# Two-layer hybrid encoder trunk on one core: group C's score products cut into two column parts, opening transfers and one table step put in another order

## The chip, the cores and the metric

The kernel runs on one core of a Trainium2 chip. The metric is device time in microseconds (us) of one execution; lower is better. TensorE (PE) multiplies, VectorE (DVE), ScalarE (ACT) and GpSimd (POOL) work elementwise, SyncE (SP) issues most of the transfers.

## The reference, cut to what matters

Two layers over 256 tokens of width 2048, all in float32. Each layer makes one projection, three groups of attention heads, a gate, an output projection and a normalised residual:

```
h = rms_norm(x, g_pre)
proj = h @ w_in                  # columns: group A, group B (low rank), group C, gates
o_a = dense attention, 8 query heads, 2 key heads, rotary, q and k normalised
o_b = low-rank attention, 4 heads, shared rotary key
o_c = neighbourhood attention, 4 heads: token t is row t // 64, column t % 64 of a grid;
      a query sees 4 rows and 16 columns around its own, plus a learned bias
y = concat(o_a, o_b, o_c) * silu(gates) @ w_out
x = x + rms_norm(y, g_post)
```

The kernel computes group C densely: all 256 keys for each query, with a bias table that holds -1e30 where the neighbourhood doesn't reach.

## The kernel before, in words

Every float32 operand is split into a high part (rounded to the reduced float32 that TensorE takes in one pass; "fp32r" in the rows) and a low part, the rest. A product of two such operands is three products on TensorE: high by high, high by low, low by high (`mm3`). Each product loads its own 128x128 stationary operand (a weight load, PEld in the rows) and streams the other one through, 512, 320 or 256 columns wide; transposes stream 128.

Weights come in tiles of 128x1024 in the order of a fixed list (`CHUNKS`), through four raw buffers (`RAW_BUFS`), issued on SP. `conv` splits a tile: ACT casts it to the high part (`whi`, line 206), DVE subtracts for the low part (`wlo`, line 207). `feed` keeps casts a few tiles ahead of the products. A chunk opens with PSUM tiles named `mm` (four buffers, two for most chunks), its products are issued, and a task (`post_...`) reads the PSUM out later; tasks advance by steps, between the products of later chunks. The order of the first chunks of layer 0 is bcq (96 products, 8 weight tiles), bckv (96 products of 320 columns), gB.0, gB.1, and so on. gB.0 takes the two PSUM tiles that bcq leaves, gB.1 those of bckv.

The opening (`start`): the input comes transposed in four pieces `xT[0]` to `xT[3]` (512 KB each); each piece is scaled by `g_pre` and split into `hT` (ACT line 209 high, DVE line 210 low, four blocks a piece). `token_factors(0)` squares the four pieces (ACT), sums them, and gets the per-token factor r with a power on POOL (line 218); r stands in every `post_` task that reads the first chunks (`while (l, "r") not in self.done`). `rstd` uses the same power on POOL.

`layer_consts(l)` loads small constants and makes four rotary tables on POOL (`c_aqn`, `s_aqn`, `c_akn`, `s_akn`, lines 327 and 329) from a rotary table (`pr`) and two gains (`g_aqn`, `g_akn`), all of them brought in on SP's queue. The tables are first used by group A (akv, aq0), long after gB. In layer 0 it is called after the sixth weight tile (`i == 5`).

A head (`head`) makes its scores into one PSUM tile `sc`, two query halves of 128 by 256 keys; in groups A and C that is 2 x 3 = 6 products of 256 columns. Group C has 4 heads a layer, 8 in all.

The order of instructions on each engine is set by a scheduler from the order and priority in the program; each engine then runs its own list in order and waits on semaphores.

Of the kernel before, what the change touches and what calls it, by code (L numbers as in the profile page):

```python
# [8 lines left out]
AF = mybir.ActivationFunctionType  # L9
# [3 lines left out]
P = 128  # L13
# [5 lines left out]
GRID_W = 64  # L19
# [143 lines left out]
class Build:  # L163
# [147 lines left out]
    def layer_consts(self, l):  # L311
        nc, d = self.nc, self.d
        g = self.tmp("gq", [P, 512], bufs=1)
        nc.sync.dma_start(g, d["bqn"][l].partition_broadcast(P))
        self.g_bq = g
        g = self.tmp("gkv", [P, 256], bufs=1)
        nc.sync.dma_start(g, d["bkvn"][l].partition_broadcast(P))
        self.g_bkv = g
        self.tab = {}
        ra = self.tmp("pr", [P, 2, 256], bufs=2)  # L320
        nc.sync.dma_start(ra, self.rope_in[:, :, :256])
        for nme in ("aqn", "akn"):
            g = self.tmp("g_" + nme, [P, 128], bufs=1)
            nc.sync.dma_start(g, d[nme][l].partition_broadcast(P))
            c = self.tmp("c_" + nme, [P, 2, 128])
            s = self.tmp("s_" + nme, [P, 2, 128])
            nc.gpsimd.tensor_tensor(c, ra[:, :, :128], g.unsqueeze(1).to_broadcast([P, 2, 128]), ALU.mult)
            for h in range(2):
                nc.gpsimd.tensor_tensor(s[:, :, 64 * h:64 * h + 64], ra[:, :, 128 + 64 * h:192 + 64 * h],
                                        g[:, 64 - 64 * h:128 - 64 * h].unsqueeze(1).to_broadcast([P, 2, 64]), ALU.mult)  # L330
            self.tab[nme] = (c, s)
# [321 lines left out]
    def head(self, l, grp, h):  # L653
        nc = self.nc
        sp = self.psum("sc", 1)
        s3 = sp.rearrange("p (q k) -> p q k", q=2)
        for qt in range(2):
            q = slice(qt * P, (qt + 1) * P)
            st = qt == 0
            if grp == "A":  # L660
                qq, kk, kv = self.qA[h // 4], self.kA, h // 4
                self.mm3(s3[:, qt], qq[0][:, h % 4, q], qq[1][:, h % 4, q], kk[0][:, kv], kk[1][:, kv], st, True)
            elif grp == "C":
                qq, kk = self.qC, self.kC
                self.mm3(s3[:, qt], qq[0][:, h, q], qq[1][:, h, q], kk[0][:, h], kk[1][:, h], st, True)
            else:
                qq, kk = self.qn, self.kn
                self.mm3(s3[:, qt], qq[0][:, h, q], qq[1][:, h, q], kk[0][:, h], kk[1][:, h], st, False)
                self.mm(s3[:, qt], self.qpe[:, h, q], self.kpe, False, False)
                self.mm(s3[:, qt], self.qpe[:, h, q], self.kpl[:, h % 2], False, True)  # L670
        yield 1
        pr = self.tmp("pr", [P, 2, 256], bufs=2)
        mx = self.tmp("mx", [P, 2], bufs=2)
        nb = self.tmp("nb", [P, 2], bufs=2)
        sm = self.tmp("sm", [P, 2], bufs=2)
        rc = self.tmp("rc", [P, 2], bufs=2)
        if grp == "C":
            for qt in range(2):
                nc.vector.scalar_tensor_tensor(pr[:, qt], s3[:, qt], self.r[:, 2 + qt:3 + qt], self.biasC[h // 2][:, h % 2, qt], ALU.mult, ALU.add)
            nc.vector.reduce_max(mx, pr, AX.X)  # L680
            nc.vector.tensor_scalar(nb, mx, -1.0, None, ALU.mult)
            for qt in range(2):
                nc.scalar.activation(pr[:, qt], pr[:, qt], AF.Exp, bias=nb[:, qt:qt + 1], scale=1.0, accum_out=sm[:, qt:qt + 1])
        else:
            nc.vector.reduce_max(mx, s3, AX.X)
            if grp == "A":
                sc = self.scA[h // 4]
                nc.vector.scalar_tensor_tensor(nb, mx, -1.0, sc[:, :, h % 4], ALU.mult, ALU.mult)  # L688
            else:
                nc.vector.tensor_scalar(nb, mx, -(192 ** -0.5), None, ALU.mult)  # L690
            for qt in range(2):
                scale = sc[:, qt, h % 4:h % 4 + 1] if grp == "A" else 192 ** -0.5
                nc.scalar.activation(pr[:, qt], s3[:, qt], AF.Exp, bias=nb[:, qt:qt + 1], scale=scale, accum_out=sm[:, qt:qt + 1])  # L693
        yield 1
        nc.vector.reciprocal(rc, sm)
        for qt in range(2):
            nc.vector.tensor_scalar(pr[:, qt], pr[:, qt], rc[:, qt:qt + 1], None, ALU.mult)
        yield 2
        pt = self.psum("tr", 2)
        for qt in range(2):  # L700
            for kt in range(2):
                self.transpose(pt[:, kt * 256 + qt * P:kt * 256 + (qt + 1) * P], pr[:, qt, kt * P:(kt + 1) * P])
        yield 1
        pT = self.tmp("pT", [P, 2, 2, 256], bufs=1)
        self.split(pt.rearrange("p (k q) -> p k q", k=2), pT[:, 0], pT[:, 1])
        yield 2
        while grp == "C" and (l, "cv") not in self.done:
            yield 1
        po = self.psum("pv", 1)
        for kt in range(2):  # L710
            if grp == "A":
                c = slice((h // 4) * P, (h // 4 + 1) * P)
                v = self.vA
            else:
                c = slice(h * P, (h + 1) * P)
                v = self.vB if grp == "B" else self.vC
            self.mm3(po[:, :256], v[0][:, kt, c], v[1][:, kt, c], pT[:, 0, kt], pT[:, 1, kt], kt == 0, kt == 1)
        yield 1
        if grp == "C":
            nc.scalar.copy(self.oC[:, h], po[:, :256])  # L720
            return
        g = {"A": lambda: self.gA[h // 4][:, h % 4], "B": lambda: self.gB[:, h]}[grp]()
        og = self.tmp("og", [P, 256], bufs=1)
        nc.vector.scalar_tensor_tensor(og, po[:, :256], 0.5, g, ALU.mult, ALU.mult)
        e = {"A": h, "B": 8 + h}[grp]
        nc.scalar.copy(self.oT[0][:, e].bitcast(F32R), og)
        nc.vector.tensor_tensor(self.oT[1][:, e].bitcast(F32R), og, self.oT[0][:, e], ALU.subtract)
# [191 lines left out]
    def start(self):  # L919
# [10 lines left out]
        self.g_pre = self.pc.tile([P, KT], F32, name="g_pre")  # L930
        xT = self.xT0 = self.unit(3) + self.unit(4)
        with self.tc.high_priority(offset=1000):
            nc.sync.dma_start(self.g_pre, self.d["gpre0"])
            x0 = lambda a, b: nc.sync.dma_start(xT[0][:, a:b], self.xT[0][:, a:b])
            x0(0, 256)
            self.load(0, self.items[0]["ncols"], lambda: x0(256, 512))
            self.load(1)
            x0(512, 1024)
            nc.sync.dma_start(xT[1], self.xT[1])
            self.load(2)  # L940
            self.load(3)
            nc.sync.dma_start(xT[2], self.xT[2])
        self.nload = 4
        self.ident = self.pc.tile([P, P], F32, name="ident")
        self.rope = self.pc.tile([P, 2, 128], F32, name="rope")
        self.mhalf = self.pc.tile([P, 8], F32, name="mhalf")
        nc.vector.memset(self.mhalf, -0.5)
        one = self.tmp("rs_a", [P, 8], bufs=2)
        nc.vector.memset(one, 1.0)
        two = self.tmp("rs_r", [P, 8], bufs=4)  # L950
        nc.gpsimd.tensor_tensor(two, one, self.mhalf, ALU.pow)
        nc.scalar.activation(two, one, AF.Exp)
        self.new_layer()
        for c in range(4):
            v = xT[c].rearrange("p (k t) -> p k t", k=4)
            for j in range(4):
                k = 4 * c + j
                self.split(v[:, j], self.hT[c][:, j, 0], self.hT[c][:, j, 1], self.g_pre[:, k:k + 1])
                if j % 2:
                    self.feed(2 * c + j // 2, 0, 0)  # L960
            if c == 1:
                nc.sync.dma_start(xT[3], self.xT[3])

    def last_chunk(self, i):

# [129 lines left out]
                nc.sync.dma_start(self.x1[m][:, h * 1024:(h + 1) * 1024], self.xt[m][h])  # L1095
        self.spawn(self.token_factors(l + 1), delay=0)
        self.layer_consts(l + 1)
        self.close_chunk(C[0])

    def run(self):  # L1100
        self.start()
        i, n = 0, len(self.items)
        while i < n:
            self.step += 1
            it = self.items[i]
            if it["name"] == "y3":
                self.last_chunk(i)
                i += 14
                continue

            self.feed(i, i, LC + min(HELD, it["ks"][0] // 2) if it["name"] == "y2" else LC)
            if it["first"]:
                self.open_chunk(it)
            self.products(it)
            if i == 5:
                self.layer_consts(0)
            if i == 2:
                self.spawn(self.token_factors(0), delay=2)
            if it["last"]:
                self.close_chunk(it)  # L1120
            self.run_tasks()
            i += 1
# [40 lines left out]
```

## Time and profile before

| what | us |
|---|---|
| median of 3 runs | 814.95 (813.52 to 815.0) |
| profiled execution | 815.99 |
| its span in the profile | 814.1 |
| PE busy in the span | 802.9 |
| DVE, ACT, POOL busy | 562.6, 436.4, 37.9 |

Busy time of PE counts an instruction until its modelled end; products overlap each other's ends, so the distance from one start to the next is what a product costs. In a timeline a row gives the start, the time from the first start to the last end, and the number of instructions merged into it.

### The profile page before, as it was taken

What the parts mean: (1) busy time and instruction counts of PE and PEld (TensorE: products, weight loads), DVE (VectorE), ACT (ScalarE), POOL (GpSimd) and SP (SyncE); (2) the same over time, 40 slices, a digit from 0 to 9 for tenths busy, and PEclk for the clock granted to TensorE, in tenths of its full rate; (3) what the DMA queues carried; (4) which work ended last, traced back from release to release, by engine and by line L of the source; (5) the groups of instructions that cost most, each with busy time, mean ns of one, the idle gap of its engine ahead of it and who ended that gap; (6) DMA issues with size and microseconds to landing.
All of it is one profiled execution on the core that took longest, in us unless ns stands there. A gap on an engine that the chain in (4) does not pass through costs nothing.

```text
span 814.1 us, 11731 instructions
## 1 busy us (share of the span) xinstructions
PE 802.9 (99%) x4345; PEld 693.1 (85%) x4345; DVE 562.6 (69%) x887; ACT 436.4 (54%) x755; POOL 37.9 (5%) x55
## 2 busy tenths in 40 slices
PE   8999999999999999999999999999999999999996
PEld 5889888888898888888898898888889988888885
DVE  6767877576777687566595776866758866874643
ACT  7455555464665555456284554645456555554531
POOL 1110000000000000200010000001000000000000
PEclk9999999999999999999999999999999999999999
DMA  8775544554445455777367455446554455566632
GB/s 290 244 253 174 200 170 161 212 203 161 170 165 181 156 185 192 258 233 254 126 216 233 157 188 198 156 156 232 182 176 161 163 175 179 184 203 211 210 126 103
DMA packets 45801, 154.59 MB, mean 190 GB/s; under 512 B 5168, under 2 KB 7600, under 8 KB 45744
## 3 DMA queue, kind: packets, MB, share of 16 engines
q1 hardware_dynamic: 43008, 144.14, 51.7%
q0 software_dynamic: 2592, 9.44, 3.6%
q8 instruction: 34, 0.56, 0.3%
q10 hardware_dynamic: 144, 0.26, 0.1%
q14 instruction: 23, 0.19, 0.1%
HBM read 149.63 MB, written 4.19 MB: 189 GB/s over the span
## 4 chain that ended last, share of the span: by engine, by line
PE 90%; DMA 3%; DVE 3%; ACT 2%; SPq 1%; issue 1%; POOL 0%; DVEq 0%; POOLq 0%; ACTq 0%
PE mm L222 80%; PE sc L222 4%; PE pv L222 3%; PE tr L231 3%; DMA wraw<-in_wts_dram 2%; DVE wlo L207 1%; ACT whi L206 1%; DMA g_akn<-in_akn_dram 1%; PE tr L222 1%; DVE u L779 1%; ACT hT L209 0%; ACT u L824 0%; SPq L274 0%; DVE hT L210 0%; DVE u L784 0%
## 5 line engine op out<-in xcount | busy, mean ns | idle before, releaser
L207 DVE TENSOR_TENSOR wlo<-wraw,whi 128x1024 fp32r<-128x1024 f32 (+2 forms) x257 | 309.0, 1204 | 158.6 <-ACT whi L206 154.6
L206 ACT CAST whi<-wraw 128x1024 fp32r<-128x1024 f32 (+2 forms) x257 | 264.9, 1033 | 216.5 <-PE mm L222 182.6
L222 PE MATMUL mm<-whi,hT 128*128 128x512 f32 (+1 forms) x768 | 232.9, 378 | 1.0 <-ACT whi L206 0.8
L222 PE MATMUL mm<-hT,whi 128*128 128x512 f32 x768 | 193.5, 394 | 1.8 <-DVE t L381 1.6
L222 PEld LDWEIGHTS mm<-whi,hT 128*128 128x128 f32 x768 | 141.6, 188 | 26.7 <-ACT whi L206 1.6
L222 PEld LDWEIGHTS mm<-hT,whi 128*128 128x128 f32 x768 | 138.2, 189 | 27.0 <-ACT whi L206 1.8
L222 PE MATMUL mm<-wlo,hT 128*128 128x512 f32 (+1 forms) x384 | 144.7, 378 | 0.9 <-DVE wlo L207 0.9
L222 PE MATMUL mm<-whi,oT 128*128 128x512 f32 x448 | 141.6, 391 | 0.0
L222 PEld LDWEIGHTS mm<-hT,wlo 128*128 128x128 f32 x768 | 104.8, 190 | 7.5
L222 PE MATMUL mm<-hT,wlo 128*128 128x256 f32 x768 | 107.1, 282 | 0.0
L222 PEld LDWEIGHTS mm<-whi,oT 128*128 128x128 f32 x448 | 84.1, 188 | 17.2
L222 PE MATMUL mm<-wlo,oT 128*128 128x512 f32 x224 | 87.2, 389 | 0.0
L222 PEld LDWEIGHTS mm<-wlo,hT 128*128 128x128 f32 x384 | 72.2, 188 | 13.8 <-DVE wlo L207 2.3
L222 PEld LDWEIGHTS mm<-wlo,oT 128*128 128x128 f32 x224 | 42.1, 188 | 8.2
L222 PE MATMUL sc<-u,u 128*128 128x256 f32 x224 | 33.7, 290 | 0.0
L693 ACT ACTIVATE pr<-sc,nb,scq 128x256 f32<-128x256 f32 x32 | 17.8, 560 | 25.0 <-DVE nb L688 25.0
L222 PEld LDWEIGHTS sc<-u,u 128*128 128x128 f32 x224 | 29.2, 190 | 0.5
L222 PE MATMUL pv<-pT,u 128*128 128x256 f32 x192 | 28.4, 284 | 0.0
L218 POOL TENSOR_TENSOR rs_r<-rs_a,mhalf 128x2 f32<-128x2 f32 (+2 forms) x12 | 15.1, 1258 | 278.0 <-DVE rs_a L217 278.0
L222 PEld LDWEIGHTS pv<-pT,u 128*128 128x128 f32 x192 | 26.5, 189 | 1.2
L352 ACT ACTIVATE junk<-mm,r 128x128 bf16<-128x128 f32 (+2 forms) x48 | 19.4, 404 | 14.6 <-DVE r L847 8.1
L352 ACT ACTIVATE junk<-mm 128x512 bf16<-128x512 f32 x16 | 9.5, 593 | 32.6 <-PE mm L222 32.6
(145 smaller groups left out, 677.7 us busy)
## 6 DMA issues: line engine op xcount, KB each, us to landing
wraw<-in_wts_dram SPq DMA_DIRECT2D x247, 512.0 KB, 3.5
wraw<-in_wts_dram SPq DMA_DIRECT2D x10, 480.0 KB, 4.6
u<-in_bias_dram POOLq DMA_DIRECT2D x4, 512.0 KB, 5.4
u<-in_x_dram POOLq DMA_DIRECT2D x4, 512.0 KB, 5.7
u<-in_gpost_dram POOLq DMA_DIRECT2D x4, 512.0 KB, 7.0
x<-u SPq DMA_DIRECT2D x4, 512.0 KB, 2.7
u<-x POOLq DMA_DIRECT2D x4, 512.0 KB, 5.4
wraw<-in_wts_dram SPq DMA_DIRECT2D x6, 256.0 KB, 3.1
```

The costliest lines, as they stand in the source:

```text
L206: nc.scalar.copy(hi.bitcast(F32R), ps)
L207: nc.vector.tensor_tensor(lo.bitcast(F32R), ps, hi, ALU.subtract)
L218: nc.gpsimd.tensor_tensor(r[:, :m], a[:, :m], self.mhalf[:, :m], ALU.pow)
L222: self.nc.tensor.matmul(out, lhsT=l.bitcast(F32R), rhs=r.bitcast(F32R), start=start, stop=stop, skip_group_check=True)
L231: self.nc.tensor.transpose(out, in_, self.ident)
L352: self.nc.scalar.activation(j[:, :n], src, AF.Square, scale=scale, accum_out=acc)
L693: nc.scalar.activation(pr[:, qt], s3[:, qt], AF.Exp, bias=nb[:, qt:qt + 1], scale=scale, accum_out=sm[:, qt:qt + 1])
L779: self.nc.vector.scalar_tensor_tensor(xc, self.q4(self.yg[m], c, n), r[:, :1], xc, ALU.mult, ALU.add)
```

## The change

Three things. In `head`, the scores of group C are made for the keys of grid columns 0 to 39 (4 rows of 40, 160 keys) and then for those of columns 40 to 63 (96 keys), each with its own `mm3`: 12 products in place of 6. The moving operand and the PSUM output become four runs with gaps. In `start`, `g_pre` moves from SP's queue to ACT's, the first half of `xT[0]` and the first weight tile come as one transfer each in place of two, ACT's first exponential (which loads its function table) stands ahead of the splits, its operand is set by POOL, and `xT[3]` is asked for with the other pieces. The four rotary tables and their transfers become a function of their own, `layer_tables`, called in layer 0 after the first weight tile of gB.1; in layer 1 it is called where the tables were made before.

```diff
@@ layer_consts
         g = self.tmp("gkv", [P, 256], bufs=1)
         nc.sync.dma_start(g, d["bkvn"][l].partition_broadcast(P))
         self.g_bkv = g
+
+    def layer_tables(self, l):
+        nc, d = self.nc, self.d
         self.tab = {}
         ra = self.tmp("pr", [P, 2, 256], bufs=2)
         nc.sync.dma_start(ra, self.rope_in[:, :, :256])
@@ head
             elif grp == "C":
                 qq, kk = self.qC, self.kC
-                self.mm3(s3[:, qt], qq[0][:, h, q], qq[1][:, h, q], kk[0][:, h], kk[1][:, h], st, True)
+
+                g = lambda a, c: a.rearrange("p (r c) -> p r c", c=GRID_W)[:, :, c]
+                for c in (slice(0, 40), slice(40, 64)):
+                    self.mm3(g(s3[:, qt], c), qq[0][:, h, q], qq[1][:, h, q], g(kk[0][:, h], c), g(kk[1][:, h], c),
+                             st and c.start == 0, True)
@@ start
         with self.tc.high_priority(offset=1000):
-            nc.sync.dma_start(self.g_pre, self.d["gpre0"])
+
             x0 = lambda a, b: nc.sync.dma_start(xT[0][:, a:b], self.xT[0][:, a:b])
-            x0(0, 256)
-            self.load(0, self.items[0]["ncols"], lambda: x0(256, 512))
+            one = self.tmp("rs_a", [P, 8], bufs=2)
+            nc.gpsimd.memset(one, 1.0)
+            nc.scalar.dma_start(self.g_pre, self.d["gpre0"])
+            x0(0, 512)
+            self.load(0)
+            two = self.tmp("rs_r", [P, 8], bufs=4)
+            nc.scalar.activation(two, one, AF.Exp)
             self.load(1)
             x0(512, 1024)
             nc.sync.dma_start(xT[1], self.xT[1])
             self.load(2)
             self.load(3)
             nc.sync.dma_start(xT[2], self.xT[2])
+            nc.sync.dma_start(xT[3], self.xT[3])
...
-            if c == 1:
-                nc.sync.dma_start(xT[3], self.xT[3])
@@ last_chunk
         self.layer_consts(l + 1)
+        self.layer_tables(l + 1)
@@ run
             if i == 5:
                 self.layer_consts(0)
+            if it["l"] == 0 and it["name"] == "gB.1" and it["first"]:
+                self.layer_tables(0)
```

On PE, at group C's first head in layer 0 (`sc` is the score tile; of the `u` tiles the first is the key, high or low part, that moves, the second the query), before:

```order
L231 MATMUL tr_3002<-ident,pr_2919 128x128 x4
L222 MATMUL sc_3011<-u_487_2344,u_545_2638 128x256
L222 MATMUL sc_3011<-u_488_2345,u_545_2638 128x256
L222 MATMUL sc_3011<-u_487_2344,u_546_2639 128x256
...
L222 MATMUL mm_2980<-hT_15_117,whi_2898 128x512 x4
```

and of the change:

```order
L231 MATMUL tr_3001<-ident,pr_2918 128x128 x4
L222 MATMUL sc_3010<-u_488_2343,u_546_2637 128x4x40
L222 MATMUL sc_3010<-u_489_2344,u_546_2637 128x4x40
L222 MATMUL sc_3010<-u_488_2343,u_547_2638 128x4x40
L222 MATMUL sc_3010<-u_488_2343,u_546_2637 128x4x24
L222 MATMUL sc_3010<-u_489_2344,u_546_2637 128x4x24
L222 MATMUL sc_3010<-u_488_2343,u_547_2638 128x4x24
...
L222 MATMUL mm_2979<-hT_16_117,whi_2897 128x512 x4
```

The three products of a query half have become six, and the neighbours in PE's list are the same; the second query half follows alike.

On POOL in layer 0 (the first two `rs_r` after the start are the token factor r and the norm of bcq, the third is the norm of bckv), before:

```order
L327 TENSOR_TENSOR c_aqn_307<-pr_303,g_aqn_305 128x256
L329 TENSOR_TENSOR s_aqn_308<-pr_303,g_aqn_305 128x2x64 x2
L327 TENSOR_TENSOR c_akn_314<-pr_303,g_akn_312 128x256
L329 TENSOR_TENSOR s_akn_315<-pr_303,g_akn_312 128x2x64 x2
L218 TENSOR_TENSOR rs_r_417<-rs_a_416,mhalf 128x2
L218 TENSOR_TENSOR rs_r_433<-rs_a_432,mhalf 128x2
L218 TENSOR_TENSOR rs_r_562<-rs_a_561,mhalf 128x2
```

and of the change:

```order
L218 TENSOR_TENSOR rs_r_400<-rs_a_399,mhalf 128x2
L218 TENSOR_TENSOR rs_r_416<-rs_a_415,mhalf 128x2
L330 TENSOR_TENSOR c_aqn_685<-pr_681,g_aqn_683 128x256
L332 TENSOR_TENSOR s_aqn_686<-pr_681,g_aqn_683 128x2x64 x2
L330 TENSOR_TENSOR c_akn_692<-pr_681,g_akn_690 128x256
L332 TENSOR_TENSOR s_akn_693<-pr_681,g_akn_690 128x2x64 x2
L218 TENSOR_TENSOR rs_r_545<-rs_a_544,mhalf 128x2
```

The tables stood ahead of all three powers and now stand between the second and the third.

On DVE in the opening, from the third weight tile's low part on (`wlo_148` is the third tile in both lists, the fifth is `wlo_169` before and `wlo_168` in the change), before:

```order
L207 TENSOR_TENSOR wlo_148<-wraw_101,whi_147 128x1024
L210 SCALAR_TENSOR_TENSOR hT_14_116<-u_4_88,g_pre,hT_14_116 128x256
L826 TENSOR_TENSOR u_48_274<-u_48_274,u_49_275 128x1024
L207 TENSOR_TENSOR wlo_158<-wraw_103,whi_157 128x1024
L210 SCALAR_TENSOR_TENSOR hT_15_117<-u_5_89,g_pre,hT_15_117 128x256 x3
L207 TENSOR_TENSOR wlo_169<-wraw_131,whi_168 128x1024
```

and of the change:

```order
L207 TENSOR_TENSOR wlo_148<-wraw_103,whi_147 128x1024
L833 TENSOR_TENSOR u_49_273<-u_49_273,u_50_274 128x1024
L207 TENSOR_TENSOR wlo_158<-wraw_105,whi_157 128x1024
L210 SCALAR_TENSOR_TENSOR hT_16_117<-u_5_89,g_pre,hT_16_117 128x256 x4
L210 SCALAR_TENSOR_TENSOR hT_17_118<-u_6_90,g_pre,hT_17_118 128x256 x3
L207 TENSOR_TENSOR wlo_168<-wraw_131,whi_167 128x1024
```

The splits of `xT[3]` (`hT_17`) have come ahead of the fifth tile's low part; before they stood three tiles later.

## Rows read from the trace of the kernel before

**Rows 1.** The page: busy time by engine, and the last chain's shares by engine.
```profile
PE 802.9 (99%) x4345; PEld 693.1 (85%) x4345; DVE 562.6 (69%) x887; ACT 436.4 (54%) x755; POOL 37.9 (5%) x55
PE 90%; DMA 3%; DVE 3%; ACT 2%; SPq 1%; issue 1%; POOL 0%; DVEq 0%; POOLq 0%; ACTq 0%
```

**Rows 2.** Stretches: length, then busy time (and instructions) of each engine.
```profile
60.00:400.00 340.00, 340.00 (x1852) 295.32 (x1853) 238.46 (x373) 182.56 (x320) 15.57 (x20) 1.00 0.55 190
420.00:806.00 386.00, 386.00 (x2088) 335.00 (x2087) 261.16 (x410) 201.71 (x345) 12.51 (x15) 1.00 0.53 180
```

**Rows 3.** Timeline of PE around a group C head.
```profile
301.67 0.88 PE L222 MATMUL sc<-u,u 128*128 128x256 f32 x6
302.39 2.00 PE L222 MATMUL mm<-hT,whi 128*128 128x512 f32 x8
...
305.18 0.60 PE L231 MATMUL tr<-ident,pr 128*128 128x128 f32 x4
305.53 2.09 PE L222 MATMUL mm<-hT,whi 128*128 128x512 f32 x8
```

**Rows 4.** Timeline of weight loads at two places.
```profile
13.39 0.30 PEld L222 LDWEIGHTS mm<-whi,hT 128*128 128x128 f32 x2 [0.34 <-ACT whi L206]
...
53.07 0.90 PEld L231 LDWEIGHTS tr<-ident,t 128*128 128x128 f32 x8
```

**Rows 5.** Groups of PE and of weight loads by shape: busy us, mean ns.
```profile
L1025 PE MATMUL tr<-u,ident 128*128 128x512 f32 x2 | 1.0, 592 | 0.0
...
L222 PEld LDWEIGHTS mm<-whi,hT 128*128 128x128 f32 x768 | 141.6, 188 | 26.7 <-ACT whi L206 1.6 <-DVE hT L210 0.6 <-ACT hT L209 0.4
...
L231 PEld LDWEIGHTS tr<-ident,t 128*128 128x128 f32 x74 | 8.6, 140 | 0.1
```

**Rows 6.** Timeline of PE near the end: one product on unreduced float32, two instructions.
```profile
805.79 1.02 PE L1025 MATMUL tr<-u,ident 128*128 128x512 f32 x2
```

**Rows 7.** Timeline of PE in the first 60 us.
```profile
26.07 0.73 PE L222 MATMUL mm<-whi,hT 128*128 128x512 f32 x2 [0.19 <-DVE hT L210]
...
45.59 0.31 PE L222 MATMUL mm<-whi,hT 128*128 128x320 f32 x1
47.51 2.08 PE L222 MATMUL mm<-hT,whi 128*128 128x512 f32 x8 [1.61 <-DVE t L381]
...
58.69 1.11 PE L222 MATMUL mm<-hT,wlo 128*128 128x256 f32 x8
59.95 2.08 PE L222 MATMUL mm<-hT,whi 128*128 128x512 f32 x8 [0.15 <-DVE t L346]
```

**Rows 8.** Timeline of POOL in the same time.
```profile
40.08 0.74 POOL L327 TENSOR_TENSOR c_akn<-pr,g_akn 128x256 f32<-128x256 f32 x1 [0.82 <-DMA g_akn<-in_akn_dram]
...
41.61 0.71 POOL L218 TENSOR_TENSOR rs_r<-rs_a,mhalf 128x2 f32<-128x2 f32 x1
...
53.05 0.70 POOL L218 TENSOR_TENSOR rs_r<-rs_a,mhalf 128x2 f32<-128x2 f32 x1 [6.67 <-DVE rs_a L217]
```

**Rows 9.** Timeline of DVE in the same time.
```profile
25.54 1.67 DVE L210 SCALAR_TENSOR_TENSOR hT<-u,g_pre,hT 128x256 fp32r<-128x256 f32 x4
...
37.50 0.17 DVE L217 TENSOR_SCALAR rs_a<-ss 128x2 f32<-128x2 f32 x1
42.36 0.17 DVE L847 COPY r<-rs_r 128x2 f32<-128x2 f32 x1 [4.69 <-POOL rs_r L218]
```

**Rows 10.** Timeline of all engines in the first 20 us.
```profile
6.39 0.73 PE L222 MATMUL mm<-whi,hT 128*128 128x512 f32 x2 [0.79 <-ACT whi L206]
...
7.00 0.62 ACT L206 CAST whi<-wraw 128x512 fp32r<-128x512 f32 x1 [0.66 <-DMA wraw<-in_wts_dram]
...
12.31 1.03 ACT L206 CAST whi<-wraw 128x1024 fp32r<-128x1024 f32 x1
...
14.65 0.50 PE L222 MATMUL mm<-wlo,hT 128*128 128x512 f32 x1 [0.53 <-DVE wlo L207]
...
18.37 1.22 DVE L207 TENSOR_TENSOR wlo<-wraw,whi 128x1024 fp32r<-128x1024 f32 x1
```

More of the change, by code (lines that the diff above doesn't have):

```diff
@@ L947, in start @@
         nc.vector.memset(self.mhalf, -0.5)
-        one = self.tmp("rs_a", [P, 8], bufs=2)
-        nc.vector.memset(one, 1.0)
         two = self.tmp("rs_r", [P, 8], bufs=4)
         nc.gpsimd.tensor_tensor(two, one, self.mhalf, ALU.pow)
-        nc.scalar.activation(two, one, AF.Exp)
         self.new_layer()
```

## The prediction

> **What bounds the kernel now.** I read the page first: PE is busy 802.9 us of the 814.1, no other engine over 70%, and PE has 90% of the last chain [rows 1]. Then the table of stretches: from 60 to 400 us and from 420 to 806 PE is busy without a break, 340.0 of 340 and 386.0 of 386 [rows 2]. All eight heads of group C lie in these stretches, so what PE gains or loses there goes into the time in full; DVE and ACT have spare time there. Outside them PE does wait: in the opening, at 45.7 us, at 59.6, and between the layers. So the change has two places to act: 48 products in the full stretches, and the first 60 us.
>
> Next I read what a product costs from start to start. Six score products of 256 columns take 301.67 to 302.39, 0.72 us, 0.120 each. From 302.39 to 305.18 there are eight of 512 columns and eight of 256; with 0.120 for the latter a 512-column one costs 0.229 [rows 3]. Half the columns, about half the price: at these widths a product costs its columns. Four transposes of 128 columns take 305.18 to 305.53, 0.088 each [rows 3], not 0.060: below 256 columns something else sets the pace.
>
> That is the weight load, one per product. Two loads whose data had just come (13.39) lie within 0.30 us [rows 4] and one lasts 0.188 [rows 5], so the second starts 0.112 after the first. Eight loads for transposes lie within 0.90, one lasts 0.140 [rows 4, 5]: (0.90 - 0.14) / 7 = 0.109. A load can start about every 0.11 us. A product of 256 columns (0.120) just covers it, one of 160 or 96 doesn't.
>
> **The change: group C's scores.** The columns stay 512 a head and high-low term; the products go from 6 to 12, so the loads go from 6 to 12. By columns alone 160 cost 0.120 x 160/256 = 0.075 and 96 cost 0.045. Both are under the load's 0.11, so I count loads: 12 x 0.112 = 1.34 us a head. One load is done under the product ahead of the group, as the transposes show: four of them took 0.35 where 4 x 0.109 = 0.44, 0.08 less. So 1.26 in place of 0.72, +0.54 a head, +4.35 us for eight. Nothing hides it, since PE has no idle time around these heads [rows 2].
>
> Bounds from both sides. Below: loads hidden entirely leaves the columns and a fixed part; from 0.229 for 512 and 0.120 for 256 the fixed part is 0.011 a product, so six more products cost 0.07 a head, +0.5 us. Above: no reduced product under 256 columns stands in the trace, and the rewritten operands have gaps; the slow row that is nearest is the product on unreduced float32 at the end, two instructions in 1.02 us of which one lasts 0.592, so 0.43 a pass [rows 5, 6] and 0.86 for 512 columns, 1.67 ns a column. At that price a head costs 6 x (0.267 + 0.160) = 2.56, +1.84, +14.7 us. I take the load's price, because its rows are of 128 columns, between 96 and 160, and have the same load per product.
>
> The Trainium skill, page "TensorE: Matmul & The Clock Gate", section "Back-to-back issue gap", gives about 81 ns a product for a sustained stream of load and product at 128 columns; by it a head would take 12 x 0.081 = 0.97, the change's cost would be an estimated +2.0 us, and the whole would end near 815.4. The same place gives about 131 ns at 512 columns where the trace has 229, so I keep to the rows.
>
> **The change: the tables.** At 45.59 the last product of bckv starts; it costs 0.15 (320/256 of 0.120). The next starts at 47.51, because DVE line 381, which empties bcq's PSUM, is late [rows 7]: 47.51 - 45.74 = 1.77 us lost. What is late behind it: the operand of the power for r is there at 37.67 (37.50 + 0.17), but POOL makes c_akn and s_akn first, which waited for g_akn, and takes it at 41.61; DVE stands 4.69 us for it until 42.36 [rows 8, 9]. With the power ahead of the tables r comes 41.61 - 37.67 = 3.9 us sooner, and so does the emptying. That is more than 1.77, so this wait goes whole. The wait at 59.95 (58.69 + 8 x 0.120 = 59.65, 0.3 us, for bckv's PSUM [rows 7]) has the same root and goes too.
>
> What is queued behind the tables now is bckv's power alone, at 53.05 before [rows 8]. g_akn is asked for behind one more weight tile on SP, which waits for the low part of gB.0's first tile. I put the end of the tables near 49 and the power near 50; line 346, 6.9 us behind the power before (53.05 to 59.95), comes at some 57, and gB.1 needs it at 57.9 (45.74 + 59.65 - 47.51). Cover of about 1 us; if it is gone, some tenths of the 0.3 stay. The transfers themselves move past weight tiles that are needed more than 10 us later.
>
> **The change: the opening.** Now the first product starts at 6.39 and the second half of the first tile is cast at 7.00, after 0.66 of waiting for its transfer [rows 10]. Whole tile in one transfer, in second place on SP's queue and not in three pieces behind g_pre: I put its landing at 6.5, from 5.8 to 7.0, so the first product at some 7.1, 0.7 later. But ACT then runs without a break to the cast of the third tile (12.31 now): one 0.43 split more and the landings some 0.4 sooner, 12.2. Its low part, which PE waits for at 14.65 [rows 10], comes at 14.5: 0.15 gained. Then DVE does an addition and the fourth tile, 1.14 each (1.22 for one such tile [rows 10], 0.08 less in a run), and seven splits at 0.42 (four take 1.67 [rows 9]) ahead of the fifth tile: 19.7. That one takes 1.22: 21.0. PE wants it 24 products of 0.227 to 0.229 after 14.5, at 20.0. So 1.0 us is lost there, and the 0.19 at 26.07, for the splits of `xT[3]` [rows 7], is gained. Sum: -0.15 + 1.0 - 0.2 = +0.65, between -0.4 (that wait doesn't show) and +1.3. ACT's table load moves ahead of the first data and g_pre to ACT's empty queue: nothing, since the first cast waits for weights anyway.
>
> **The sum.** +4.35 - 1.77 - 0.3 + 0.6 = +2.9 us. The profiled execution took 815.99, so 818.9; the median lies 1.04 lower, so 817.8.
>
> **The rivals.** First, the narrow products run at the slow price. For it: every reduced product in the trace has 256 columns or more, and moving operand and output now have gaps. Against: from 512 to 256 the price falls evenly, with no step. At the unreduced product's 1.67 ns a column: 814.95 + 14.7 - 1.5 = 828.2. At one of its passes, 0.83 ns, 160 columns cost 0.133 and 96 the load's 0.112: 1.47 a head, +6.0, 819.5. The Trainium skill has a rule for such a slower write: page "Advanced Engine Details and Errata", section "PSUM Cachelines", says that any non-contiguous pattern slows matmuls significantly, and that pairs of elements should be contiguous, which runs of 40 and 24 keep; no row here shows a product with gaps.
>
> Second, on the other side: the loads are pulled ahead far enough to hide. Then a head costs +0.07, the change +0.5, and the opening decides: 814.95 + 0.5 - 1.5 = 814.0, no slower. It decides from about 0.085 us a load down, where 12 loads give +2.4. For it: the four transposes at 0.088. Against: eight in a row from 53.07 keep 0.109.
>
> Third, the opening's gain is lost: the splits of `xT[3]` cost 1.0 us or more and bckv's power is late, so that 1.77 becomes a later wait elsewhere. Then 819.3 or more.
>
> **How the numbers follow.** Load price with the opening's gain 0.50 (its own range 816.3 to 819.3); slow price 0.25 whole and 0.07 half; loads hidden or nearly so 0.12; opening's gain lost 0.06. 0.2% is 1.6 us, about what a measurement here can tell from no change. Slower is the first case beyond 816.6 (about 0.42), both slow prices and the third: 0.78. Same: the rest of the first and most of the hidden loads, 0.18. Faster 0.04. The range goes from 815.4, within the hidden loads, to 829.5, past the slow price, since leaving that out would leave out more than 2 in 10.
>
> **What would show it.** Right: a group C head's 12 products within some 1.2 to 1.35 us from first start to the next product; weight loads there about 0.11 apart; the first product of gB.0 directly behind bckv's last; a wait of about 1 us on DVE line 207 near 20 us. Wrong: 2.5 us a head (slow price), 0.8 (loads hidden), or a new wait on PE near 57 us for line 349 (346 before).

## The result, and the profile after

| what | before | after |
|---|---|---|
| median, us | 814.65 (4 runs, 813.52 to 815.0) | 819.82 (4 runs, 819.68 to 820.88) |
| profiled execution, us | 815.99 | 819.85 |
| its span | 814.1 | 818.1 |

The ratio is 1.0072, with a 95% interval of 1.0059 to 1.0086 (the two medians alone give 1.0063): the change makes the kernel 5.2 us slower by the medians, 3.9 by the two profiled executions. The forecast was 817.8, slower by 2.9.

The page of the changed kernel, busy time by engine and the last chain by engine; these lines answer to [rows 1]:

```profile
PE 806.8 (99%) x4393; PEld 697.9 (85%) x4393; DVE 565.4 (69%) x886; ACT 437.4 (53%) x755; POOL 42.3 (5%) x56
...
PE 94%; DVE 2%; DMA 1%; ACT 1%; issue 0%; SPq 0%; DVEq 0%; POOLq 0%; POOL 0%; ACTq 0%
```

The 48 more products and loads are there (4393 for 4345), and PE is still the bound. POOL is busy 4.4 us longer with the same tables. PE's timeline at the places that the prediction spoke of, in the opening and around the group C head of [rows 3]:

```profile
6.12 0.74 PE L222 MATMUL mm<-whi,hT 128*128 128x512 f32 x2 [0.79 <-ACT whi L206]
...
13.92 0.50 PE L222 MATMUL mm<-wlo,hT 128*128 128x512 f32 x1 [0.53 <-DVE wlo L207]
20.09 0.50 PE L222 MATMUL mm<-wlo,hT 128*128 128x512 f32 x1 [0.40 <-DVE wlo L207]
...
45.02 0.31 PE L222 MATMUL mm<-whi,hT 128*128 128x320 f32 x1
45.17 2.00 PE L222 MATMUL mm<-hT,whi 128*128 128x512 f32 x8
...
56.27 1.11 PE L222 MATMUL mm<-hT,wlo 128*128 128x256 f32 x8
59.26 2.08 PE L222 MATMUL mm<-hT,whi 128*128 128x512 f32 x8 [1.88 <-DVE t L349]
...
301.57 1.43 PE L222 MATMUL sc<-u,u 128*128 128x160 f32 x12
302.84 2.09 PE L222 MATMUL mm<-hT,whi 128*128 128x512 f32 x8
304.77 1.11 PE L222 MATMUL mm<-hT,wlo 128*128 128x256 f32 x8
```

The row of twelve names the wider form; six of the twelve have 96 columns. The weight loads there, before:

```profile
302.27 1.70 PEld L222 LDWEIGHTS mm<-hT,whi 128*128 128x128 f32 x8
```

and after:

```profile
301.45 1.43 PEld L222 LDWEIGHTS sc<-u,u 128*128 128x128 f32 x12
302.80 1.70 PEld L222 LDWEIGHTS mm<-hT,whi 128*128 128x128 f32 x8
```

Twelve loads lie within 1.43, and one lasts 0.19: they are (1.43 - 0.19) / 11 = 0.113 apart.

Three readings of PE's rows. The head's twelve products take 301.57 to 302.84, 1.27 us, where six took 0.72; the eight 512-column products behind them take 1.93 (to 304.77) where they took 1.84 before (302.39 to 305.18, less 0.95 for the eight narrow ones [rows 3]). gB.0 starts directly behind bckv's last product, at 45.17 and not at 47.51 as in [rows 7]: 2.3 us gained there. But gB.1 starts at 59.26 in place of 59.95: a new wait of 1.88 us for DVE line 349 (346 before) has eaten all but 0.7 of it.

The span can be put together from this. From gB.1's start to the unreduced product near the end (805.79 before [rows 6], 810.09 after) PE needs 750.8 us in place of 745.8, 5.0 more, all of it group C; the opening gives 0.7, the tail 0.3 (8.3 us behind that product before, 8.0 after). That is the 4.0 of the spans.

Where the new wait comes from is read on three engines. SP's waits between 28 and 62 us (who waited for whom: total, times, longest), two that are new:

```profile
SPq L327 <- POOL s_aqn L332: 3.1, 1, 3.1
...
SPq L327 <- POOL s_akn L332: 2.4, 1, 2.4
```

SP's own timeline in that stretch (the issue, not the transfer):

```profile
45.78 0.33 SPq L327 DMA_DIRECT2D g_aqn<-in_aqn_dram  x1
46.21 0.60 SPq L274 DMA_DIRECT2D wraw<-in_wts_dram  x1
49.28 0.33 SPq L327 DMA_DIRECT2D g_akn<-in_akn_dram  x1
49.70 1.33 SPq L274 DMA_DIRECT2D wraw<-in_wts_dram  x3
```

These `g_aqn` and `g_akn` are those of layer 1, fetched ahead. Each has one buffer, so it must wait until the tables of layer 0 have read the old one, and the tables are now late. Behind each stands a weight tile of gB.1, the second and the third, issued at 46.21 and 49.70. POOL's timeline, the four tables:

```profile
42.50 1.44 POOL L330 TENSOR_TENSOR c_aqn<-pr,g_aqn 128x256 f32<-128x256 f32 x1 [1.94 <-DMA g_aqn<-in_aqn_dram]
43.90 1.85 POOL L332 TENSOR_TENSOR s_aqn<-pr,g_aqn 128x128 f32<-128x128 f32 x2
45.72 1.72 POOL L330 TENSOR_TENSOR c_akn<-pr,g_akn 128x256 f32<-128x256 f32 x1
47.40 1.86 POOL L332 TENSOR_TENSOR s_akn<-pr,g_akn 128x128 f32<-128x128 f32 x2
49.23 0.69 POOL L218 TENSOR_TENSOR rs_r<-rs_a,mhalf 128x2 f32<-128x2 f32 x1
```

The third tile's cast on ACT, and what follows on DVE:

```profile
55.10 1.05 ACT L206 CAST whi<-wraw 128x1024 fp32r<-128x1024 f32 x1 [3.31 <-DMA wraw<-in_wts_dram]
```

```profile
56.18 1.23 DVE L207 TENSOR_TENSOR wlo<-wraw,whi 128x1024 fp32r<-128x1024 f32 x1 [3.14 <-ACT whi L206]
57.33 0.22 DVE L345 TENSOR_TENSOR t<-mm,rope 128x64 f32<-128x64 f32 x1
...
59.04 0.21 DVE L349 TENSOR_TENSOR t<-t,t 128x64 f32<-128x64 f32 x1
```

bckv's power was done at 49.92, but the lines that empty its PSUM stand in DVE's list behind the low part of gB.1's third tile. DVE stood 3.14 us for that tile's cast and ran line 349 only at 59.04. From the cast's start to PE's start is 59.26 - 55.10 = 4.16. In the trace before it is 4.16, too (59.95 [rows 7]), by that tile's cast and DVE's wait for it:

```profile
55.79 1.05 ACT L206 CAST whi<-wraw 128x1024 fp32r<-128x1024 f32 x1 [1.02 <-DMA wraw<-in_wts_dram]
```

```profile
56.87 1.22 DVE L207 TENSOR_TENSOR wlo<-wraw,whi 128x1024 fp32r<-128x1024 f32 x1 [0.84 <-ACT whi L206]
```

The cast starts when the transfer lands. PE could have started at 57.22 (56.27 and 0.95 for eight narrow products): 2.04 us are lost, and in this trace any cast after about 53.1 costs time.

### The profile page after: what moved, and what is told of

It is laid out like the page before. It is cut to its first block, busy times and chain, and to the rows that moved or that the text cites. A ratio compares the mean times of both kernels' runs of the same rounds, so it can differ in the third digit from the quotient of the medians.

```text
span 818.1 us, 11826 instructions
## 1 busy us (share of the span) xinstructions
PE 806.8 (99%) x4393; PEld 697.9 (85%) x4393; DVE 565.4 (69%) x886; ACT 437.4 (53%) x755; POOL 42.3 (5%) x56
## 4 chain that ended last, share of the span: by engine, by line
PE 94%; DVE 2%; DMA 1%; ACT 1%; issue 0%; SPq 0%; DVEq 0%; POOLq 0%; POOL 0%; ACTq 0%
PE mm L222 83%; PE sc L222 4%; PE pv L222 3%; PE tr L231 3%; DMA wraw<-in_wts_dram 1%; DVE wlo L207 1%; PE tr L222 1%; DVE u L786 1%; ACT whi L206 0%; ACT hT L209 0%; DVE hT L210 0%; ACT u L831 0%; DVE u L791 0%; DVE hT L207 0%; ACT junk L355 0%
## 5 line engine op out<-in xcount | busy, mean ns | idle before, releaser
L222 PE MATMUL sc<-u,u 128*128 128x256 f32 (+2 forms) x272 | 38.1, 284 | 0.0
L222 PEld LDWEIGHTS sc<-u,u 128*128 128x128 f32 x272 | 34.2, 190 | 0.5
```

Source lines behind the costliest of these rows:

```text
L222: self.nc.tensor.matmul(out, lhsT=l.bitcast(F32R), rhs=r.bitcast(F32R), start=start, stop=stop, skip_group_check=True)
```

## The experiments

My theory, after the traces: the cut costs 5.0 and nothing else does in the full stretches; the opening's gain went into the new wait, by way of SP's queue. Nothing of the computation is left out in any of these kernels.

**The cut alone.** Before, with the diff's part in `head` and nothing else.

> The kernel before with the cut of group C's scores alone. Theory (each product pays a weight load of 0.11 us, nothing hides it): a group C head takes 1.27 to 1.35 us in place of 0.72, as in the changed kernel's trace, so +4.4 to +4.9 us, 819.0 to 819.6. Rival (the cut costs more, and part of it is paid back where PE waits anyway): under +4. Rival (the opening costs nothing and the cut explains the whole +5.2): +5.2 or more.

Measured 818.95 (818.19 to 819.68) beside 813.97 for before (812.66 to 815.85) on the same chip: ratio 1.0063 (1.005 to 1.0075), +5.0. By that interval the cut alone costs 4.1 to 6.1 us, so it is enough for the whole change; the other two parts together give back nothing that shows. From gB.1's start to the end PE needs 750.8 us here as well.

**The opening and the tables alone.** The change with the scores as before.

```
-  g = lambda a, c: ...   (and the loop over two column parts)
+  self.mm3(s3[:, qt], qq[0][:, h, q], qq[1][:, h, q], kk[0][:, h], kk[1][:, h], st, True)
```

> The changed kernel with group C's scores as before: the opening and the tables alone. Theory (the 1.77 us wait at 45.7 went, 0.5 came from the first products, and 1.9 came back as a wait at 57.4 for bckv's PSUM): -0.7 us, 813.7 to 814.3, which hardly differs from the kernel before. Rival (the whole 1.5 that the prediction counted): 813.1 or less. Rival (the opening costs time): above 815.

Measured 816.26 (814.13 to 819.47), ratio 1.0029 (1.0016 to 1.0042): slower than before, where I had expected it level with it. The profiled execution has a wait of 1.93 us for line 349, and behind it this, in stretches (length, then busy time and instructions of PE, PEld, DVE, ACT, POOL, then PE's granted clock, DMA share, GB/s):

```profile
58.00:60.00 2.00, 1.27 (x6) 1.09 (x7) 2.00 (x9) 1.82 (x5) 0.00 (x0) 1.00 0.68 244
60.00:62.00 2.00, 2.00 (x9) 1.77 (x8) 2.00 (x3) 1.94 (x3) 0.00 (x0) 0.55 0.17 47
62.00:64.00 2.00, 2.00 (x9) 1.76 (x8) 1.58 (x2) 0.32 (x1) 0.00 (x0) 0.59 0.91 271
64.00:66.00 2.00, 2.00 (x14) 1.78 (x14) 0.22 (x1) 0.78 (x1) 0.00 (x0) 1.00 0.73 193
```

After the wait the granted clock falls to the lower level (1.2 of 2.4 GHz) for some 3 us, and eight products of 256 columns take 1.91 us in place of 1.11. From gB.1's start to the end this execution needs 747.4, without the drop 745.8: the wait of 1.93 costs 1.6 more. The twelve runs fit this: in the five up to 815.02 us the mean granted clock was 0.998 to 0.999, in the seven from 815.91 up 0.995 to 0.997. So the scatter is put down to a wait that in some executions brings the clock down, though only one execution was seen in a trace. It also means that the parts don't add up: alone the opening and the tables cost 2.3 us by the medians, beside the cut about 0.2, and in the changed kernel's trace the clock stayed.

**Two buffers for the gains.** The change with one edit.

```
-            g = self.tmp("g_" + nme, [P, 128], bufs=1)
+            g = self.tmp("g_" + nme, [P, 128], bufs=2)
```

> The changed kernel with two buffers for each of the gains g_aqn and g_akn, so that layer 1's transfers of them, which stand in SP's list between gB's weight tiles, no longer wait for the tables on POOL. Theory (SP is held by these two transfers for 3.1 and 2.4 us, the sixth and seventh weight tiles after bckv come late, DVE waits for their low parts and comes late to line 349, which frees bckv's PSUM): the wait of 1.9 us on PE at 57.4 goes, -1.5 to -1.9 us against the changed kernel, some 818.1. Rival (bckv's power, behind the tables on POOL until 49.2, is what is late): nothing changes, 819.8.

Measured 817.77 (817.21 to 817.84), 2.05 below the changed kernel by the medians (measured on two chips; each against before on its own chip, the loss is 3.8 in place of 5.2). SP's order is the same, and its waits for POOL are gone. The third tile's cast starts at 51.52 and PE has no gap (ACT's timeline, and the stretch with its busy times):

```profile
51.52 1.05 ACT L206 CAST whi<-wraw 128x1024 fp32r<-128x1024 f32 x1 [1.86 <-PE tr L231]
```

```profile
45.00:60.00 15.00, 15.00 (x91) 13.31 (x91) 11.33 (x25) 8.80 (x17) 5.26 (x7) 1.00 0.75 245
```

So SP's hold by the gains is what makes the wait in the changed kernel. The power of bckv stands behind the tables here as there, so the rival that blamed POOL's order falls.

**Keys cut without gaps.** The change with keys 0 to 159 and 160 to 255, so that moving operand and output are contiguous (its scores read the same keys in another grouping).

```
-                for c in (slice(0, 40), slice(40, 64)):
-                    self.mm3(g(s3[:, qt], c), ... g(kk[0][:, h], c), g(kk[1][:, h], c),
+                for c in (slice(0, 160), slice(160, 256)):
+                    self.mm3(s3[:, qt, c], ... kk[0][:, h, c], kk[1][:, h, c],
```

> The changed kernel with the keys cut into 0 to 159 and 160 to 255, so the same widths of 160 and 96 columns without gaps in operand or output. Theory (the weight load sets the pace): the same 1.27 to 1.35 us a head, the time of the changed kernel within 0.1 us per head. Rival (the gaps cost): under 1.1 us a head, 1.5 us or more below the changed kernel.

Measured 821.24 (819.64 to 824.36). The time says nothing of gaps, since its profiled execution has a wait of 4.18 us for line 349 and the lower clock until 67 us; why that wait is longer here isn't known. The head does:

```profile
306.13 1.43 PE L222 MATMUL sc<-u,u 128*128 128x160 f32 x12
307.41 2.07 PE L222 MATMUL mm<-hT,whi 128*128 128x512 f32 x8
```

1.28 us a head, as with gaps (1.27). Runs of 40 and 24 elements cost nothing here.

**Four parts.** Keys in four contiguous parts of 64, so 24 products a head.

```
+                for c in (slice(0, 64), slice(64, 128), slice(128, 192), slice(192, 256)):
```

> The changed kernel with group C's keys in four contiguous parts of 64: 24 products and 24 weight loads a head, the columns unchanged. If the load sets the pace, a head takes 24 x 0.112 - 0.08 = 2.6 us from its first product to the next group, with loads 0.11 apart, and the time is about 10.8 us over the changed kernel's 819.8: 830 to 832. Rival: a product costs its columns and a fixed part. From 0.229 at 512 columns and 0.120 at 256 the columns are 0.060 for 128; the twelve products of the changed kernel took 0.106 each at 128 on average, so the fixed part would be 0.046, and 64 columns would cost 0.076: 1.8 us a head, and 823.5 to 825.

Measured 832.78 (829.96 to 835.12), ratio 1.0218 (1.0193 to 1.0242). The head on PE, and its loads:

```profile
307.40 2.76 PE L222 MATMUL sc<-u,u 128*128 128x64 f32 x24
309.99 2.10 PE L222 MATMUL mm<-hT,whi 128*128 128x512 f32 x8
```

```profile
307.27 2.77 PEld L222 LDWEIGHTS sc<-u,u 128*128 128x128 f32 x24
```

2.59 us a head, where the load's price gave 2.6 and columns with a fixed part 1.8. With 0.19 for the last, the loads are (2.77 - 0.19) / 23 = 0.112 apart. The total lies 0.8 over the expected 830 to 832; its profiled execution has a wait of 4.38 us for line 349 and the lower clock until 67 us. At 64, 96 and 160 columns it is the load that is paid.

**The tables back.** The change with `layer_tables(0)` again directly behind `layer_consts(0)`; the cut and the opening's transfers stay.

> The changed kernel with the table step put back to where it stood (after the sixth weight tile): the cut of group C and the opening's transfers stay. If the table step behind gB.1's first tile makes the wait for line 349 (by holding SP), that wait is gone here, the wait for line 381 near 45 us is back at 0.6 to 2.4 us (the transfers bring PE there up to 0.6 sooner), and the time is that of the cut alone, 818.2 to 819.4. Rival: the opening's transfers make the new wait (the splits of the fourth piece come ahead of the fifth tile); then the wait for 349 stays and the time is 819.8 or more. The prediction's price of the transfers, +0.6, would show as 819.5, unless the wait for line 381 absorbs it.

Measured 819.32 (817.06 to 821.18). The time is the cut's, but the wait that I expected near 45 us isn't there and the one that I expected gone is. In the profiled execution, the third tile's cast on ACT, and PE:

```profile
55.02 1.05 ACT L206 CAST whi<-wraw 128x1024 fp32r<-128x1024 f32 x1 [1.93 <-DMA wraw<-in_wts_dram]
```

```profile
59.19 2.09 PE L222 MATMUL mm<-hT,whi 128*128 128x512 f32 x8 [1.78 <-DVE t L349]
```

No wait of SP for POOL shows here. The theory is too narrow: the hold by the gains is one way to a late third tile, and with the tables back and the opening's transfers rewritten there is a second.

**The tables moved alone.** Before with the third part of the change only, one buffer for the gains.

> Before, with the table step moved and nothing else: one buffer for the gains, opening and scores as before. Theory A, the moved tables alone make the wait for line 349, because the next layer's gains stand in SP's list among gB.1's tiles and wait for the tables: SP waits 2 to 3 us each for POOL, PE waits 1 us or more for line 349, and the time is 815 to 817, some 2 to 3 us over the kernel with two gain buffers (813.1). Theory B, it takes the opening's transfers as well (they change SP's list, too): SP waits, but its tiles stand in another order, PE's wait is 0.5 at most, and the time 812.8 to 814.

Measured 812.96 (812.78 to 813.31, 11 runs) beside 813.88 (813.02 to 816.86): ratio 0.9985 (0.9977 to 0.9994), under the 0.2% that can be told, with hardly any scatter. Theory B holds. SP waits for POOL as in the change, 2.0 and 2.1 us; but its list, from SP's timeline, reads

```profile
43.06 0.33 SPq L274 DMA_DIRECT2D wraw<-in_wts_dram  x1
43.43 0.43 SPq L314 DMA_DIRECT2D gq<-in_bqn_dram  x1
44.19 0.33 SPq L274 DMA_DIRECT2D wraw<-in_wts_dram  x1
46.65 0.33 SPq L327 DMA_DIRECT2D g_aqn<-in_aqn_dram  x1
49.16 0.33 SPq L327 DMA_DIRECT2D g_akn<-in_akn_dram  x1
49.58 0.38 SPq L274 DMA_DIRECT2D wraw<-in_wts_dram  x1
```

gB.1's second and third tiles (43.06, 44.19) stand ahead of both gains; in the change they stand one behind each. PE starts gB.1 at 56.92 without a wait. It takes both, the opening's rewritten transfers and the late tables, to put those tiles behind a held buffer.

**The tables back, with more buffers.** The kernel with the tables back, once with two buffers for the gains and once with two for `gq` (with three for the squares `ss` in place of four, to make the space).

> The changed kernel with the table step back where it stood and two buffers for the gains. With the step back the tables end before SP comes to the next layer's gains, so a second buffer takes no wait away: PE still waits 1 to 2.5 us for line 349 and the time stays near 819.3, as with the step back and one buffer. Rival: what held SP there was the gain's transfer after all (it took 1.95 us to issue in that trace); then the wait for 349 goes and the time is 817.5 to 818.2.

> The changed kernel with the table step back where it stood and two buffers for gq, the next layer's copy of which stands in SP's list ahead of gB.1's tiles and waits for line 384 (2.2 us, until 44.2 us); the squares' small tile has three buffers in place of four to make the space. The instructions of every engine stand as before this edit. If that hold makes gB.1's tiles late, SP issues them about 2 us sooner, PE's wait for line 349 falls from 1.8 to 0.3 or nothing, and the time is 817.5 to 818.3 in place of 819.3. Rival: the tiles are late because the DMA engines are full or the raw buffers come free late; then the wait stays above 1 us and the time at 819.

Measured 818.95 (817.89 to 821.74) and 819.21 (818.28 to 820.77), beside 819.32 for one buffer each on another chip: no difference that shows in either. With two gain buffers the profiled execution, the fastest of its six, has no wait for 349 (cast at 53.05, gB.1 at 57.21, again 4.16 later). With two for `gq` SP no longer waits for line 384, but the cast starts at 54.53 and PE waits 1.33. There the hold on `gq` isn't the cause, and the rival, tiles that land late, fits: ACT waits 2.96 us for a transfer. Why they land later with these opening transfers isn't settled.

**The tables moved, with two gain buffers.** Once with the opening as before, once with the change's opening; scores as before in both.

> Before, with the table step moved behind gB.1's first tile and two buffers for the gains; scores and opening as before. If the wait for line 381 is what scatters the time before (812.7 to 815.9), and SP's wait for the gains is what made the table step cost, both are gone: 812.5 to 813.4 with little scatter, and PE with no wait from 27 to 400 us. Rival: the table step still disturbs (POOL's tables take twice as long beside DVE, bckv's power comes late), a wait for line 349 of some tenths or more shows, and the time is 814 or more.

> The changed kernel's opening and table step, two buffers for the gains, scores as before: the change without the cut and with SP's wait taken away. Theory: 817.8 of the kernel with two gain buffers less the cut's 5.0 by that trace, 812.5 to 813.1, the fastest of all, with a narrow scatter. If the opening's transfers cost the 0.6 that the prediction counted, it is slower by that than the kernel with the opening as before; if they gain what the trace suggests (bckv's last product 45.0 in place of 45.6), it is the faster by up to 0.6. Rival: the time stays near 814, since something else than the waits sets it.

Measured 813.06 (812.55 to 813.84), ratio 0.9979 (0.997 to 0.9989), and 812.93 (812.05 to 813.13), ratio 0.9974 (0.9964 to 0.9984), beside 814.69 for before (812.81 to 817.45). Both as the theory said: no wait between 21 and 400 us, little scatter, 1.6 to 1.8 us under before. The stretch of the second kernel, PE busy throughout:

```profile
21.00:400.00 379.00, 379.00 (x2084) 330.83 (x2083) 269.97 (x420) 202.64 (x349) 24.00 (x29) 1.00 0.58 196
```

The 0.13 between the two can't be told from nothing, so beside late tables and two buffers the opening's transfers cost or bring nothing that shows. The last of these kernels, the change without its cut and with a second buffer, has the lowest median, but it can't be told from the tables moved alone (812.96 on another chip).

**Before, once more.** The unchanged kernel, a second profiled execution.

> The kernel before, unchanged, profiled once more. If the wait of 1.77 us for line 381 is one execution's and not the kernel's, it differs here, between 0 and 2 us, and the time goes with it: 814.2 plus the sum of the waits for 381 and 346, to within 0.6. If it is the kernel's own, it is again 1.6 to 1.8 and the time near 816.

```profile
44.67 0.31 PE L222 MATMUL mm<-whi,hT 128*128 128x320 f32 x1
45.22 2.06 PE L222 MATMUL mm<-hT,whi 128*128 128x512 f32 x8 [0.23 <-DVE t L381]
```

813.27 us, span 811.4: 2.7 less than the execution ahead of the prediction. bckv's last product starts 0.9 sooner, gB.0 loses 0.4 (44.67 + 0.15 to 45.22) and not 1.77, and there is no wait for line 346. The sum in the expectation (814.2 and the waits) was off by 1.2, twice what it allowed: bckv's last product, ahead of both waits, came 0.9 sooner. That the wait of 1.77 isn't a fixed part of the kernel is shown.

## Why the prediction was right or wrong

**The cut: right in mechanism, a little small.** The forecast was 1.26 us a head and +4.35 in all. In the changed kernel the heads take 1.27 six times and 1.35 and 1.36 for the first of each layer, 10.3 us in place of 5.9: +4.4. The missing part is behind the head, where the next eight 512-column products take 1.93 in place of 1.84. The load of the first of them starts 0.04 ahead of it (302.80 and 302.84), before the change 0.12 (302.27 and 302.39): the 0.08 less of lead is nearly the whole difference. Without waits on either side (the two kernels with two gain buffers, cut and uncut) PE needs 750.7 and 745.8 from gB.1's start to the end: 4.9, 0.61 a head.

**The rivals on the price.** All other prices of a head in the prediction (2.56, 1.47, 0.97 and 0.8) fall with 1.27, and gaps cost nothing by the kernel without them. The Trainium skill, page "Advanced Engine Details and Errata", section "PSUM Cachelines", says that any non-contiguous pattern slows matmuls significantly; for runs of 40 and 24 float32 elements the measurement decides otherwise, 1.27 with gaps and 1.28 without.

**The waits gained: mis-sized, in two ways.** The prediction counted -1.77 - 0.3 from one profiled execution. That one took 815.99, more than any of the three runs beside it. In the second execution the same two waits sum to 0.4, and the kernels with the tables moved and no new wait gain 0.9 to 1.8 by the medians. The step that made the sum against that execution's own 815.99 and then moved it to the median by 1.04 kept the whole gain of 2.07, though, by the second execution, part of the 1.04 was these very waits.

**The step that failed is the cover for bckv's PSUM.** The prediction put line 349 "6.9 us behind the power" at some 57, and priced its failure at "some tenths of the 0.3"; a new wait for line 349 near 57 us stood in its list of what would show it wrong, and came, 1.88 us long. The power came at 49.23, as forecast; line 349 came at 59.04. The 6.9 us were no chain from the power. In the trace before, too, DVE stood 0.84 us for the third tile of gB.1 in between, and gB.1 starts 4.15 to 4.17 us after that tile's cast in every trace with the wait. With it goes the sentence that the transfers of the tables "move past weight tiles that are needed more than 10 us later". I counted layer 0's own transfers, and not that layer 1's copies of the same constants already stood in SP's list, in single buffers that the tables hold. The nearest rival, the third, had 0.06: its later wait came, but by another way, since bckv's power was on time.

**The opening: off in its parts, small in the sum.** The forecast was +0.6. The first product came at 6.12, not 7.1; the third tile's low part is waited for until 13.92, not 14.5; a wait for line 207 shows at 20.09, 0.40 of idle time by the row where I had 1.0. With the waits behind it gone, the kernels with the old and the new opening lie 0.13 apart: nothing in place of +0.6. Over all traces bckv's last product starts at 44.57 to 45.59 with the old opening (five) and at 44.32 to 45.30 with the new one (nine), so the 0.6 between the first two traces is no more than scatter. The tail's 0.3 does show in every trace, 8.0 with the new opening and 8.3 to 8.4 with the old; why isn't known.

**The sum.** By the medians: cut +5.0 where +4.35 was forecast, opening and tables beside it about +0.2 where -1.5 was. The measured 819.82 lies past 819.3, the end of the range that the prediction gave to its likeliest case; the whole range covers it because it reached to 829.5 for the slow price. The changed kernel's own trace shows no fall of the clock behind its 1.88; some other kernels with that wait do. The +0.6 that didn't come made up for part of the gain that didn't come either: that is luck.

## What to carry to other kernels

Cutting a product into narrower ones pays for the load of its stationary operand each time, once the columns no longer cover it; count loads, and the one behind the group. Before a step is moved, list what stands behind its buffers on the transfer queue, the copies fetched ahead for a later layer too: a single buffer that is read later holds every transfer behind it in that list. A wait in one profiled execution is worth what a second execution also shows.

## What the runs showed of the hardware

GpSimd slows beside VectorE. A table on POOL takes 0.74 and 0.88 us for its two kinds while DVE stands still ([rows 8] and the row below, beside the wait of 4.69 in [rows 9]), and 1.44 to 1.86 beside DVE's subtractions, above.

```profile
40.78 0.88 POOL L329 TENSOR_TENSOR s_akn<-pr,g_akn 128x128 f32<-128x128 f32 x2
```

In the kernel with the tables moved alone one trace has both, 1.85 beside DVE and 0.86 while DVE waits:

```profile
44.77 1.85 POOL L332 TENSOR_TENSOR s_aqn<-pr,g_aqn 128x128 f32<-128x128 f32 x2
...
48.27 0.86 POOL L332 TENSOR_TENSOR s_akn<-pr,g_akn 128x128 f32<-128x128 f32 x2
```

VectorE pays less steadily. In the changed kernel three of the four subtractions beside the tables took 1.49 to 1.76 in place of 1.22 (the longest is shown); in the kernel with the tables moved alone the two beside them took 1.24. Why isn't known.

```profile
43.25 1.76 DVE L207 TENSOR_TENSOR wlo<-wraw,whi 128x1024 fp32r<-128x1024 f32 x1
```

The Trainium skill, page "GPSIMD Engine Reference", section "Specifications", says that POOL's interfaces to SBUF are shared with VectorE, with contention with DVE instructions in a 2-port mode or with two SBUF inputs. DVE's subtractions here have two such inputs, and POOL's 1.85 and 0.86 agree.

In the traces the granted clock fell in or after a wait of 1.93 us in one kernel and of 4.2 to 4.4 in two others, to the lower level, and came back 3 to 7 us later; after 1.88, 1.78 and 1.33 it stayed. In the keys cut without gaps the fall took another 2.2 us (753.0 from gB.1's start to the end against 750.8).
